# Sharing the second layer's modulation among VectorE and TensorE, and regrouping the products of a scan step

## The chip, the cores and the metric

One core of one Trainium2 chip runs the whole program in one launch. The metric is the device time of one execution in microseconds. A core has TensorE (PE; its weight loads are shown apart as PEld), VectorE (DVE), ScalarE (ACT), GpSimd (POOL) and SyncE (SP), each with a queue of its own; transfers between HBM and SBUF are issued from the queues of SP and ScalarE here.

## The reference

Two layers, with different weights, over 384 tokens of width 1024: 128 context tokens and 256 latent tokens. Each layer is a mixer and a feed-forward, and both are modulated by a condition vector `c` (one for the context, one for the latents):

```python
m = silu(c) @ w_mod + b_mod                # w_mod: 1024 x 6144, per layer
sh_m, sc_m, gt_m, sh_f, sc_f, gt_f = split(m, 6)
h = rms_norm(x) * (1 + sc_m) + sh_m
x = x + gt_m * rms_norm(mixer(h))          # four branches; one is a recurrent scan
h = rms_norm(x) * (1 + sc_f) + sh_f
f = (silu(h @ w_gate) * (h @ w_up)) @ w_down   # hidden width 2816
x = x + gt_f * rms_norm(f)
```

The scan of one mixer branch runs, per token, over a 64 x 64 state `S` per head and direction:

```python
s_a = S @ (-kk)
S = S * w + outer(s_a, kk * a) + outer(v, k)
y = S @ r
```

## The kernel before, in words

Activations lie with channels on the partitions and the 384 tokens along the free side. Every large product is made of three matmuls: weights and activations are split into a high part (rounded to fp32r) and a low part, and high x high, high x low and low x high are summed in PSUM (L684 to L686; the first stage of each sublayer has its own lines L706 to L708). Weights come from HBM in units of up to 512 KB into a ring of three raw buffers (`fetch`, L387); ScalarE copies each half unit to its high part (L417), VectorE or GpSimd subtracts to the low part (L419), four halves ahead of their use. The order of all units is a list made in advance (`layer_plan`).

A layer goes: first products of the mixer; a gate stage of 32 gate tiles (b, m), in which two side programs, attention and the scan, are woven between the gate products slot by slot (`run`, `paced`); the output projection; a bridge (norm and residual); the feed-forward's loop over 22 tiles, of which the first three are made in the bridge and tiles 3 to 21 in `ffn_main`, each a gate product, an up product and `hidden` (L1762 to L1767); the down projection (`out_gemm`, eight tiles, evacuated at L1548 and L1551); and a bridge.

The modulation is 48 output tiles of 128 rows per layer (eight tiles for each of the six parts). Layer 0's tiles 0 to 39 are made on TensorE: 0 to 15 at the start, and 16 to 39 in mixer 0, one step after each of the first 24 gate tiles, each 128 of the 1024 inputs of eight tiles (`mod_step`, `mod_mm` L515): four fp32 matmuls, 32 columns of `c` standing, 256 columns of raw weights moving, each of two passes. After eight steps ScalarE copies the bank (L542), and two steps later two transposes (L549) and an add of the bias (L553) put it in place. Such a unit sits in the ring of raw weights like any other.

The other 56 tiles (layer 0's 40 to 47 and all 48 of layer 1) are made on VectorE in layer 0's feed-forward: `mod_some` fetches the next n units of 512 KB through SP's queue into three buffers `rawm` and, placed behind the last instruction of the tile, multiplies the units fetched the call before with the two conditions, with a running sum (`mod_vector`, L561). It fetches two units a tile in `ffn_main` and three a tile in the down projection, until 56 are done. The conditions stand broadcast over the partitions in `cb`.

A scan works on chunks of 32 tokens, for a pair of heads at a time (two pairs a layer). Step i treats n = 4 sequences (two groups, two directions) for i < 4 and n = 2 for i >= 4. It forms `ry` from a state product (L1409, 64 x 64) and a score product (L1414, 32 x 64), for the two heads of the pair (`par`) on partitions 0 to 63 and 64 to 127, all in one PSUM bank; VectorE copies it to `rs` (L1417); a product with `qt` (L1425) gives `UV`; then the state update (L1435) and the last score (L1442). Before, the first part went sequence by sequence: for each `idx`, two state products, then two score products. An fp32 matmul is two passes.

Of the kernel before, what the change touches and what calls it, by code (L numbers as in the profile page):

```python
# [18 lines left out]
L = 2  # L19
# [27 lines left out]
REST = (5, 6, 7, 7)  # L47
YORD = (0, 1, 2, 3, 5, 4, 6, 7)
# [36 lines left out]
def layer_plan(l):  # L85
# [17 lines left out]
    for i in range(len(tiles) + LAG):  # L103
        if i == 8:
            for n in ("cq0", "cq1", "ckv"):
                z(n)
        if i < len(tiles):
            z("gate%d_%d" % tiles[i])
            if l == 0 and i < 24:
                mod(l, 1 + i // 16, i % 16)  # L110
        if i >= LAG:
            b, m = tiles[i - LAG]
            if m % 2 == 1:
                out.append(("br", l, (b, m // 2), 0, 2, 256))
# [136 lines left out]
def host_arrays(w):  # L251
    def by_partition(a):

        return a.reshape(*a.shape[:-1], KD, 128).swapaxes(-1, -2).reshape(a.shape)
# [5 lines left out]
    for l in range(L):  # L260
# [45 lines left out]
                         for i in range(16)]),  # L306
        "wm1": by_partition(np.concatenate([w["w_mod"][0].T.reshape(48, 128, D)[40:],
                                            w["w_mod"][1].T.reshape(48, 128, D)])),
# [17 lines left out]
def build(tc, I, O):  # L326
# [231 lines left out]
    def mod_vector(l, t, cb, acc, raw, junk):  # L558

        for g in range(2):  # L560
            V.scalar_tensor_tensor(junk, raw, 1.0, cb[:, g, :], op0=OP.mult, op1=OP.mult,  # L561
                                   accum_out=acc[:, t, g:g + 1])
# [215 lines left out]
    def mixer(l, x, xspill, hs, M, merged_of):  # L778
# [67 lines left out]
        def main():  # L846
# [9 lines left out]
            for i in range(len(tiles) + LAG):  # L856
# [3 lines left out]
                if i < len(tiles):  # L860
                    b, m = tiles[i]
                    yield from gemm(("z", l, "gate%d_%d" % (b, m)), hz, gate_evac(b, m))
                    if l == 0 and i < 24:
                        mod_step(l, 1 + i // 16, i % 16)
                        yield
# [352 lines left out]
        def rwkv_pair(pr):  # L1218
# [178 lines left out]
            for i in range(8):  # L1397
# [5 lines left out]
                for idx in range(n):  # L1403
                    g, d = IDX[idx]
                    c = chunk(g, d, i)

                    for par in range(2):
                        rows = slice(par * 64, par * 64 + 64)
                        T.matmul(ry[rows, idx, :], kr_[rows, d, c, :], sS[rows, idx, :], start=(idx == 0),  # L1409
                                 stop=False, skip_group_check=True)  # L1410
                    for par in range(2):
                        rows = slice(par * 64, par * 64 + 64)
                        lo = slice(par * 64 + 32, par * 64 + 64)
                        T.matmul(ry[rows, idx, :], am[lo, d, c, :], uv[lo, s0 + idx, :], start=False,  # L1414
                                 stop=(idx == n - 1), skip_group_check=True)
# [114 lines left out]
    def out_gemm(kind, l, xs, q, x, work, ztag, acc_tags, tags, stats=True, extra=None):  # L1530
# [40 lines left out]
        for m in range(8):  # L1571
# [8 lines left out]
            if extra:  # L1580
                extra(end[0])
# [122 lines left out]
    for l in range(L):  # L1704
# [18 lines left out]
        with tc.tile_pool(name=f"ffn{l}", bufs=1) as M:  # L1723
            if l + 1 < L:
                load_params(l + 1)
                scale_params(l + 1)
                load_rest(l + 1)
                cb = M.tile([128, 2, D], F32, name="cb")
                dma(cb, bass.AP(tensor=csd.tensor, offset=csd.offset, ap=[[0, 128], [D, 2], [1, D]]))
                acc = M.tile([128, 56, 2], F32, name="acc")  # L1730
                todo = list(range(56))

                def add_bias(l, n, t):

                    t0 = t + 1 - n
                    m0 = t0 + 40 if l == 0 else t0 - 8
                    b = PAR[l]["vec"][:, V_BMOD + m0:V_BMOD + m0 + n, None]
                    V.tensor_add(mod_tile(l)[:, m0:m0 + n, :], acc[:, t0:t + 1, :], b.to_broadcast([128, n, 2]))

                there = []  # L1740

                def mod_some(n, behind):

                    with tc.issue_after(behind.ins):
                        for t, raw in there:
                            junk = M.tile([128, D], F32, name="junk", tag="junk")
                            mod_vector(1, t, cb, acc, raw, junk)
                            if t == 7:
                                add_bias(0, 8, t)
                            elif t % 16 == 7:  # L1750
                                add_bias(1, 16, t)
                    there.clear()
                    for t in todo[:n]:
                        raw = M.tile([128, D], F32, name="rawm", tag="rawm", bufs=3)
                        dma(raw, I["wm1"][t])
                        there.append((t, raw))
                    del todo[:n]
# [13 lines left out]
            def ffn_main():  # L1771
# [5 lines left out]
                for m in range(3, FM):  # L1777
# [5 lines left out]
                    if l + 1 < L:  # L1783
                        mod_some(2, ins)

            drive(ffn_main())
            cnt["pool"] = POOL_FFN[l] - 1 if l == 0 else 1
            last = l + 1 == L
            mg, ps = out_gemm("down", l, hid, post_scale(l, 1), x, M, "z", ("sq0", "sq1", "sq2"), ("th",), not last,
                              None if last else lambda ins: mod_some(3, ins))  # L1790
# [31 lines left out]
```

## Time and profile before

| what | value |
|---|---|
| median of 3 runs | 1647.55 us (1641.81 to 1648.14) |
| the profiled execution | 1648.67 us, span 1646.9 us |
| mean granted TensorE clock | 0.974 |
| PE busy | 1563.0 us (95%), 10774 matmuls |
| DVE busy | 1065.8 us (65%) |
| ACT busy | 634.7 us (39%) |
| POOL busy | 484.1 us (29%) |
| the chain that ended last | PE 34%, DVE 5%, POOL 1% |
| modulation on VectorE (L561) | 112 x 1592 ns, 178.3 us |

Times are counted from the span's start. A matmul's shown duration overlaps with the next one's, so a cost on TensorE is read from start to start. The windows view gives, for a stretch, its length, then the busy us of PE, PEld, DVE, ACT and POOL with their instruction counts, the granted clock (1.00 is 2.4 GHz, 0.50 is 1.2 GHz), the busy share of the DMA engines and the GB/s they moved. A wait is put down to what ended it.

### The profile page before, as it was taken

To read this page: it belongs to the slowest core of one execution; us is meant where nothing else is said; L and a number is where in the kernel's file an instruction comes from. 1 tells how busy PE (TensorE), PEld (TensorE's weight loads), DVE (VectorE), ACT (ScalarE), POOL (GpSimd) and SP (SyncE) were. 2 spreads that over 40 slices of the span, in tenths; PEclk is the share of its full clock that TensorE was granted. 3 is DMA by queue.
4 is the path that set the end of the run, shared out by engine and by line. 5 is a ranking of instruction groups with operands and counts; after the bars stand their busy time and mean duration, and the time that the engine had idled before them with its cause. 6 is when DMAs were issued, how large, how long until landed. Compare 5 with 4: busy or idle time off the path is not lost. (4 is left out here: it accounts for less than half of the span.)

```text
span 1646.9 us, 28089 instructions
## 1 busy us (share of the span) xinstructions
PE 1563.0 (95%) x10774; PEld 1410.4 (86%) x10774; DVE 1065.8 (65%) x2258; ACT 634.7 (39%) x1361; POOL 484.1 (29%) x357
## 2 busy tenths in 40 slices
PE   8999999999999998888888999999999999999997
PEld 7988778777898998888888888788779999999997
DVE  5477358844567699997996586488545677444333
ACT  3463334432343432223324553344333435444331
POOL 3110001101236465553545110011112354333222
PEclk9999899999998999998999999999999979999998
DMA  9544233425541565556644442223223414333342
GB/s 334 187 136 136 67 127 112 133 84 156 161 158 59 196 215 200 195 194 203 211 161 137 128 120 82 62 83 96 74 68 119 154 61 132 128 128 128 119 128 74
DMA packets 106615, 224.25 MB, mean 136 GB/s; under 512 B 41264, under 2 KB 51568, under 8 KB 105712
## 3 DMA queue, kind: packets, MB, share of 16 engines
q1 hardware_dynamic: 79696, 136.52, 25.7%
q10 hardware_dynamic: 26784, 85.93, 16.0%
q8 instruction: 85, 1.39, 0.3%
q14 instruction: 50, 0.41, 0.1%
HBM read 213.33 MB, written 9.08 MB: 135 GB/s over the span
## 5 line engine op out<-in xcount | busy, mean ns | idle before, releaser
L417 ACT ACTIVATE whi<-raw 128x512 fp32r<-128x512 f32 (+2 forms) x580 | 343.6, 602 | 460.5 <-PE bank L685 279.7
L684 PE MATMUL bank<-hk,whi 128*128 128x384 f32 x1424 | 503.2, 354 | 1.6 <-DVE mg L1551 1.1
L685 PE MATMUL bank<-hk,whi 128*128 128x384 f32 x1424 | 483.2, 339 | 2.0 <-DVE hk L1521 2.0
L684 PEld LDWEIGHTS bank<-hk,whi 128*128 128x128 f32 x1424 | 269.6, 189 | 25.9 <-issue 15.5
L685 PEld LDWEIGHTS bank<-hk,whi 128*128 128x128 f32 x1424 | 269.7, 189 | 6.8 <-DVE hk L1521 3.2
L561 DVE SCALAR_TENSOR_TENSOR junk<-rawm,cb 128x1024 f32<-128x1024 f32 x112 | 178.3, 1592 | 0.9
L684 PE MATMUL bank<-hid,whi 128*128 128x384 f32 x352 | 121.3, 345 | 6.3 <-DVE th L1763 6.3
L685 PE MATMUL bank<-hid,whi 128*128 128x384 f32 x352 | 121.0, 344 | 0.0
L684 PEld LDWEIGHTS bank<-hid,whi 128*128 128x128 f32 x352 | 68.2, 194 | 6.6 <-DVE th L1763 6.6
L708 PE MATMUL bank<-hk,whi 128*128 128x384 f32 x192 | 62.9, 341 | 5.6 <-DVE hk L616 5.2
L685 PEld LDWEIGHTS bank<-hid,whi 128*128 128x128 f32 x352 | 68.0, 193 | 0.0
L706 PE MATMUL bank<-hk,whi 128*128 128x384 f32 x192 | 65.6, 342 | 1.9 <-ACT hk L608 1.6
L1558 POOL TENSOR_TENSOR acc<-acc,sqo 128x384 f32<-128x384 f32 x42 | 54.7, 1309 | 43.1 <-ACT sqo L1554 23.3
L1766 ACT ACTIVATE hid<-th 128x384 fp32r<-128x384 f32 x44 | 23.1, 526 | 111.5 <-DVE th L1764 110.1
L889 POOL TENSOR_TENSOR merged<-merged,gate 128x384 f32<-128x384 f32 x24 | 30.3, 1263 | 107.1 <-DVE gate L888 88.7
L1767 DVE TENSOR_TENSOR hid<-th,hid 128x384 fp32r<-128x384 f32 x44 | 36.9, 839 | 22.5 <-ACT hid L1766 22.5
L841 ACT ACTIVATE gate<-bank 128x384 f32<-128x384 f32 x64 | 31.0, 484 | 52.2 <-PE bank L686 39.9
L1417 DVE COPY rs<-bank 128x256 f32<-128x256 f32 (+1 forms) x32 | 11.5, 358 | 56.3 <-PE bank L1414 56.3
L909 ACT ACTIVATE prob<-bank,tiny 128x384 f32<-128x384 f32 (+1 forms) x56 | 27.1, 485 | 44.8 <-DVE tiny L908 42.4
L708 PEld LDWEIGHTS bank<-hk,whi 128*128 128x128 f32 x192 | 35.8, 188 | 7.9 <-DVE hk L616 6.2
L888 DVE SCALAR_TENSOR_TENSOR gate<-gate,bank 128x384 f32<-128x384 f32 x48 | 26.3, 550 | 22.9 <-PE bank L882 22.6
L706 PEld LDWEIGHTS bank<-hk,whi 128*128 128x128 f32 x192 | 36.5, 190 | 3.7 <-ACT hk L608 2.1
(2019 smaller groups left out, 3674.5 us busy)
## 6 DMA issues: line engine op xcount, KB each, us to landing
raw<-in_w ACTq DMA_DIRECT2D x126, 512.0 KB, 3.6
raw<-in_w SPq DMA_DIRECT2D x108, 512.0 KB, 3.9
rawm<-in_wm SPq DMA_DIRECT2D x56, 512.0 KB, 3.6
raw<-in_w SPq DMA_DIRECT2D x41, 384.0 KB, 3.1
wm<-in_wm SPq DMA_DIRECT2D x16, 512.0 KB, 8.0
raw<-in_w ACTq DMA_DIRECT2D x32, 256.0 KB, 2.7
raw<-in_w ACTq DMA_DIRECT2D x15, 384.0 KB, 3.4
bt<-in_bt SPq DMA_DIRECT2D x8, 256.0 KB, 4.5
```

The costliest lines, as they stand in the source:

```text
L417: last_split[:] = [S.activation(hi[:, :w], raws[i][:, sl], AF.Copy)]
L561: V.scalar_tensor_tensor(junk, raw, 1.0, cb[:, g, :], op0=OP.mult, op1=OP.mult, accum_out=acc[:, t, g:g + 1])
L684: T.matmul(ps[:, :n], wh, xh, start=(k == 0), stop=False)
L685: T.matmul(ps[:, :n], wh, xl, start=False, stop=False)
L706: T.matmul(o, wh, xh, start=(i == 0), stop=False)
L708: T.matmul(o, wh, xl, start=False, stop=(i == 7))
L841: S.activation(gates[b, m], ps[:, :NT], AF.Tanh, scale=0.5)
L888: V.scalar_tensor_tensor(gt, gt, 1.0, ps[:, :NT], op0=OP.add, op1=OP.mult)
L889: (G if m % 2 else V).tensor_add(merged[:, m, :], merged[:, m, :], gt)
L909: S.activation(e[:, :n], src, AF.Exp, bias=nb, scale=scale, accum_out=sm)
L1558: (V if i == 1 else G).tensor_add(a, a, b)
L1767: last = V.tensor_sub(h[:, 1, :], th, h[:, 0, :].bitcast(F32))
```

## The change

The modulation of layer 1 is shared out. VectorE keeps 32 tiles: in layer 0's feed-forward layer 0's 40 to 47 and layer 1's 0 to 15, in layer 1's feed-forward layer 1's 40 to 47. Layer 1's tiles 16 to 39 are made on TensorE in mixer 1, by the same steps as layer 0's in mixer 0; their units now stand in the ring of raw weights. `mod_some` fetches two units at every third tile of `ffn_main` and one at the others, and no longer runs in the down projection. In a scan step all state products are issued first, then all score products.

```diff
+VMOD = [(0, m) for m in range(40, 48)] + [(1, m) for m in range(16)] + [(1, m) for m in range(40, 48)]
+VMOD_IN = (range(0, 24), range(24, 32))
...
-            if l == 0 and i < 24:
+            if i < 24:
                 mod(l, 1 + i // 16, i % 16)
...
-                    if l == 0 and i < 24:
+                    if i < 24:
                         mod_step(l, 1 + i // 16, i % 16)
                         yield
...
-                for idx in range(n):
-                    g, d = IDX[idx]
-                    c = chunk(g, d, i)
-
-                    for par in range(2):
-                        rows = slice(par * 64, par * 64 + 64)
-                        T.matmul(ry[rows, idx, :], kr_[rows, d, c, :], sS[rows, idx, :], start=(idx == 0),
-                                 stop=False, skip_group_check=True)
-                    for par in range(2):
-                        rows = slice(par * 64, par * 64 + 64)
-                        lo = slice(par * 64 + 32, par * 64 + 64)
-                        T.matmul(ry[rows, idx, :], am[lo, d, c, :], uv[lo, s0 + idx, :], start=False,
-                                 stop=(idx == n - 1), skip_group_check=True)
+                todo = [(idx, IDX[idx][1], chunk(*IDX[idx], i), par) for idx in range(n) for par in range(2)]
+                for idx, d, c, par in todo:
+                    rows = slice(par * 64, par * 64 + 64)
+                    T.matmul(ry[rows, idx, :], kr_[rows, d, c, :], sS[rows, idx, :], start=(idx == 0),
+                             stop=False, skip_group_check=True)
+                for idx, d, c, par in todo:
+                    rows = slice(par * 64, par * 64 + 64)
+                    lo = slice(par * 64 + 32, par * 64 + 64)
+                    T.matmul(ry[rows, idx, :], am[lo, d, c, :], uv[lo, s0 + idx, :], start=False,
+                             stop=(idx == n - 1), skip_group_check=True)
...
-                todo = list(range(56))
...
+            todo = list(VMOD_IN[l])
...
+                for t in todo[:n]:
+                    raw = M.tile([128, D], F32, name="rawm", tag="rawm", bufs=3)
+                    dma(raw, I["wm1"][t])
+                    there.append((t, raw))
+                del todo[:n]
...
-                    if l + 1 < L:
-                        mod_some(2, ins)
+                    mod_some(2 if m % 3 == 0 else 1, ins)
...
-            mg, ps = out_gemm("down", l, hid, post_scale(l, 1), x, M, "z", ("sq0", "sq1", "sq2"), ("th",), not last,
-                              None if last else lambda ins: mod_some(3, ins))
+            mg, ps = out_gemm("down", l, hid, post_scale(l, 1), x, M, "z", ("sq0", "sq1", "sq2"), ("th",), not last)
```

## Rows read from the trace of the kernel before

**Rows 1.** windows: length, busy PE, PEld, DVE, ACT, POOL; clock, DMA, GB/s

```profile
577.67:585.99 8.32, 8.32 (x50) 8.32 (x49) 7.69 (x12) 3.33 (x8) 5.30 (x3) 1.00 0.63 201
577.67:741.92 164.25, 144.94 (x790) 140.71 (x788) 154.10 (x194) 49.05 (x98) 92.26 (x48) 0.97 0.58 201
741.92:763.30 21.38, 15.13 (x72) 14.88 (x71) 16.42 (x24) 5.50 (x11) 5.51 (x4) 0.76 0.63 208
763.30:846.50 83.20, 73.67 (x398) 71.45 (x397) 79.59 (x109) 26.23 (x49) 42.91 (x28) 0.96 0.60 199
1402.76:1535.88 133.12, 133.12 (x770) 133.12 (x769) 57.04 (x80) 54.96 (x98) 41.65 (x32) 1.00 0.38 126
1535.88:1551.60 15.72, 15.72 (x92) 15.72 (x91) 6.07 (x9) 5.75 (x12) 2.60 (x2) 1.00 0.34 102
1551.60:1621.30 69.70, 69.70 (x398) 69.70 (x397) 22.45 (x39) 23.74 (x44) 15.12 (x14) 1.00 0.38 123
```

**Rows 2.** tanh of the gate/up loop, each layer: count, ns, first and last start

```profile
L1762 ACT ACTIVATE th<-bank x17: 468/472/474, 577.7 to 741.9; 128x384 f32<-128x384 f32 x17
...
L1762 ACT ACTIVATE th<-bank x17: 472/472/472, 1402.8 to 1535.9; 128x384 f32<-128x384 f32 x17
```

**Rows 3.** TensorE's waits, layer 0 feed-forward: total us, times, longest

```profile
PE bank L684 <- DVE th L1763: 6.3, 1, 6.3
PE bank L686 <- DVE wlo__8214 L419: 2.5, 1, 2.5
```

**Rows 4.** modulation products: groups of instructions (busy, mean ns), and their durations

```profile
L561 DVE SCALAR_TENSOR_TENSOR junk<-rawm,cb 128x1024 f32<-128x1024 f32 x112 | 178.3, 1592 | 0.9
...
L561 DVE DVE_READ_ACCUMULATOR junk<-rawm,cb 128x1 f32 x112 | 8.8, 78 | 0.0
...
L561 DVE SCALAR_TENSOR_TENSOR junk<-rawm,cb x112: 1208/1219/2329, 575.3 to 859.9; 128x1024 f32<-128x1024 f32 x112
```

**Rows 5.** windows view: gate stages of mixers 0 and 1, a stretch of 0

```profile
144.10:469.70 325.60, 320.78 (x2616) 257.70 (x2617) 183.59 (x480) 118.76 (x269) 45.28 (x36) 0.98 0.41 124
991.30:1294.00 302.70, 297.28 (x2434) 249.64 (x2433) 181.62 (x483) 116.21 (x266) 45.82 (x37) 1.00 0.29 87
174.11:184.35 10.24, 10.24 (x65) 8.02 (x62) 3.63 (x10) 2.92 (x7) 0.00 (x0) 0.50 0.08 27
```

**Rows 6.** TensorE in order of time, a modulation step: start us, us, count

```profile
158.22 0.33 PE L685 MATMUL bank<-hk,whi 128*128 128x384 f32 x1
158.39 0.34 PE L686 MATMUL bank<-hk,wlo__1832 128*128 128x384 f32 x1
158.66 0.64 PE L515 MATMUL bank<-raw,cs 128*32 128x256 f32 x8
159.23 0.45 PE L684 MATMUL bank<-hk,whi 128*128 128x384 f32 x1
```

**Rows 7.** transposes of the modulation in mixer 0: count, duration ns min/median/max

```profile
L549 PE MATMUL bank<-cst,mt x6: 271/273/329, 276.8 to 437.4; 128*128 128x128 f32 x6
```

**Rows 8.** TensorE in order of time, one scan step of four products

```profile
154.88 0.33 PE L1409 MATMUL bank<-S,KR 64*64 64x64 f32 x4
155.14 0.33 PE L1414 MATMUL bank<-UV,AM 32*64 32x64 f32 x4
...
156.97 0.45 PE L684 MATMUL bank<-hk,whi 128*128 128x384 f32 x1
```

**Rows 9.** TensorE in order of time, blocks of one kind, 16 and 8 passes

```profile
1023.08 0.68 PE L1435 MATMUL bank<-UV,BKT 64*64 64x64 f32 x16
1023.69 0.63 PE L1442 MATMUL bank<-UV,AM 32*32 32x64 f32 x14
...
213.52 0.45 PE L1435 MATMUL bank<-UV,BKT 64*64 64x64 f32 x8
213.90 0.41 PE L1442 MATMUL bank<-UV,AM 32*32 32x64 f32 x8
```

**Rows 10.** ScalarE's waits in mixer 0's gate stage: total us, times, longest

```profile
ACT whi L417 <- DMA raw<-in_w: 24.9, 16, 4.8
```

More of the change, by code (lines that the diff above doesn't have):

```diff
@@ L306, in host_arrays @@
                          for i in range(16)]),
-        "wm1": by_partition(np.concatenate([w["w_mod"][0].T.reshape(48, 128, D)[40:],
-                                            w["w_mod"][1].T.reshape(48, 128, D)])),
+        "wm1": np.stack([by_partition(w["w_mod"][l].T.reshape(48, 128, D)[m]) for l, m in VMOD]),
         "x": x.T.reshape(KD, 128, NT).transpose(1, 0, 2),
@@ L556, in mod_place, with mod_vector @@
         return last
-    def mod_vector(l, t, cb, acc, raw, junk):
+    def mod_vector(t, cb, acc, raw, junk):
         for g in range(2):
@@ L1528, in drive, with out_gemm @@
             pass
-    def out_gemm(kind, l, xs, q, x, work, ztag, acc_tags, tags, stats=True, extra=None):
+    def out_gemm(kind, l, xs, q, x, work, ztag, acc_tags, tags, stats=True):
         ps2, ps3 = bk_rw(), bk_o()
@@ L1579, in out_gemm @@
                     sums(6)
-            if extra:
-                extra(end[0])
         with tc.issue_after(main_mm[0].ins):
@@ L1727, in build @@
                 load_rest(l + 1)
-                cb = M.tile([128, 2, D], F32, name="cb")
-                dma(cb, bass.AP(tensor=csd.tensor, offset=csd.offset, ap=[[0, 128], [D, 2], [1, D]]))
-                acc = M.tile([128, 56, 2], F32, name="acc")
-                todo = list(range(56))
[L1733 to L1757, printed above, removed]
+            cb = M.tile([128, 2, D], F32, name="cb")
@@ new lines, in build, with add_bias, mod_some @@
+            dma(cb, bass.AP(tensor=csd.tensor, offset=csd.offset, ap=[[0, 128], [D, 2], [1, D]]))
+            acc = M.tile([128, len(VMOD), 2], F32, name="acc")
+            todo = list(VMOD_IN[l])
+            def add_bias(t):
+                (ml, m0), t0 = VMOD[t - 7], t - 7
+                b = PAR[ml]["vec"][:, V_BMOD + m0:V_BMOD + m0 + 8, None]
+                V.tensor_add(mod_tile(ml)[:, m0:m0 + 8, :], acc[:, t0:t + 1, :], b.to_broadcast([128, 8, 2]))
+            there = []
+            def mod_some(n, behind):
+                with tc.issue_after(behind.ins):
+                    for t, raw in there:
+                        junk = M.tile([128, D], F32, name="junk", tag="junk")
+                        mod_vector(t, cb, acc, raw, junk)
+                        if t % 8 == 7:
+                            add_bias(t)
+                there.clear()
+                for t in todo[:n]:
[3 more added lines that the diff above has]
+                del todo[:n]
@@ L1782, in ffn_main @@
                     ins = hidden(m, *got)
-                    if l + 1 < L:
-                        mod_some(2, ins)
+                    mod_some(2 if m % 3 == 0 else 1, ins)
             drive(ffn_main())
+            assert not todo and not there
             cnt["pool"] = POOL_FFN[l] - 1 if l == 0 else 1
             last = l + 1 == L
-            mg, ps = out_gemm("down", l, hid, post_scale(l, 1), x, M, "z", ("sq0", "sq1", "sq2"), ("th",), not last,
-                              None if last else lambda ins: mod_some(3, ins))
+            mg, ps = out_gemm("down", l, hid, post_scale(l, 1), x, M, "z", ("sq0", "sq1", "sq2"), ("th",), not last)
             if last:
```

## The prediction, made before the change was run

> **What bounds the kernel now.** I read the page's engine shares and clock line first, then cut the span into stages with the windows view, then compared the same stage of the two layers, then the waits of TensorE, and last the instructions in order of time. The two layers run the same program on the same shapes, so one layer's stage is a measured stand-in for the other's.
>
> The two feed-forward stages differ most [rows 1, 2]. From the fourth to the last gate/up tile there are 17 tanh instructions, so 16 tiles, in both layers. Layer 1 takes 133.1 us, 8.32 us a tile, TensorE busy without a hole and VectorE 57.0 us. Layer 0 takes 164.3 us, 10.27 us a tile, VectorE busy 154.1 us: 9.63 of each 10.27. The down projection repeats it: 21.38 us to its first tile against 15.72, then 83.20 us for six tiles against 69.70. TensorE's waits in these stages name VectorE each time: one of 6.3 us for `th`, and ten of 1.9 to 2.5 us for a low half of the weights (L419), of which the longest is shown [rows 3]. So in layer 0 VectorE sets the pitch, and what fills it is the modulation: 112 products of 1.59 us, each with an accumulator read of 0.08 us, 1.67 us together [rows 4]. In layer 1's feed-forward TensorE sets the pitch.
>
> In the gate stage of both mixers TensorE sets it: busy 320.8 of 325.6 us in layer 0, 297.3 of 302.7 us in layer 1 [rows 5]. An instruction added there costs its time, one removed gives it back, less what then waits.
>
> **The change part by part.** The sum is made against the profiled execution, 1648.67 us (span 1646.9, 1.8 us around it); the median of the runs is 1647.55, 1.1 lower.
>
> (a) *Gate/up of layer 0.* The loop fetched 38 units of two products; now it fetches 24: two at every third tile, one at the others, and multiplies them a tile later. A tile now carries 4 products, 6.68 us of VectorE's 9.63, which leaves 2.95 for its own work. Afterwards three tiles carry 8 products, 13.4 us, and 3 x 2.95 = 8.9: 22.2 us against 3 x 8.32 = 25.0 of TensorE. The one tile in three that keeps four products asks for 9.63, 1.3 us over the pitch; the two after it ask for 6.29 and leave 2.0 each. That such an overhang is swallowed is seen in the first tile that carried four products: VectorE did 7.69 of the 9.63 asked, and the tile still took 8.32 [rows 1]. So TensorE's pitch returns and the stage takes 133.1: **-31.1 us**. Late next is TensorE itself. If the cover failed in every one of the six heavy tiles, 6 x 1.3 = 8 us would come back: bounds -31.1 and -23.
>
> (b) *Down projection of layer 0.* Its 18 units go altogether, with the two left over from the loop. The stretch to the first tile falls by 5.7 us, the next six tiles by 13.5: **-19.2 us**. The last tile is left as it is, since it carried no product. The layer-0 stage also squares and sums for the next norm, which layer 1 doesn't; that may keep 2 us of it: bounds -19.2 and -17.
>
> (c) *Modulation in mixer 1.* 24 steps of four matmuls (eight passes) are added, and three pairs of transposes, three copies on ScalarE and three small adds on VectorE. In mixer 0 the same step lies between an L686 that begins at 158.39 and an L684 at 159.23, 0.84 us where two neighbouring matmuls are 0.17 apart (158.22 to 158.39): 0.67 us a step, 24 x 0.67 = 16.1 [rows 6]. Six transposes at 0.27 us add at most 1.6 [rows 7]. That makes 17.7. From above: mixer 0's gate stage is 22.9 us longer than mixer 1's [rows 5], but it holds a stretch of 10.24 us at a granted clock of 0.50, the lower level, 1.2 GHz, which costs at most half of itself, 5.1; 22.9 - 5.1 = 17.8. I take **+18.0**, bounds 16.1 (transposes hidden) and 22.9. The 24 transfers of 512 KB move from SP's queue to ScalarE's, where each waits until TensorE has read the unit three before it. Queued behind it are the copies that split the weights and the evacuations of PSUM, and TensorE waits for both. In mixer 0, which has the same order, ScalarE waits 24.9 us for such transfers in 16 waits [rows 10], yet TensorE is busy 98.5% of the stage; so I cost the move at nothing beyond the 22.9. SP loses 32 transfers in layer 0 and gains 8 in layer 1.
>
> (d) *Order in the scan step.* A step of four products reads state, score, state, score, eight blocks, from 154.88 to the next matmul at 156.97: 2.09 us, 0.26 a block, and so 1.04 us for the four blocks of a two-product step [rows 8]. Blocks of one kind run closer: 16 passes of L1435, the same 64x64 shape, take 0.61 us from start to the next kind, 8 passes 0.38 [rows 9]. The 32x64 scores have no such row; the nearest are L1435 and the 32x32 L1442, 14 passes of which last 0.63 us where 16 of L1435 last 0.68, so I take 0.61 and 0.38 for them too. A four-product step then takes 1.22 us, 0.87 less, a two-product step 0.76, 0.28 less. There are 16 of each (two pairs of heads, two layers): 13.9 + 4.5 = 18.4 us. Between blocks VectorE and ScalarE work for the attention side, and they lose up to 0.87 us of cover a step; I give a tenth back: **-16.5**, bounds -18.4 and nothing (the instructions are the same, so no loss).
> Here a rule speaks against the change. The Trainium skill, TensorEngine Tiling (Array Packing), section Gotcha 1: PSUM Pressure, says that different row tiles cannot access one PSUM bank at the same time; the two heads of a pair are such row tiles, and here they write one bank. By it grouping would overlap nothing and (d) would be about nothing. The L1435 rows disagree: its passes write one bank at 0.61/16 = 0.04 us each, the mixed blocks at 0.26/4 = 0.065.
>
> (e) *Feed-forward of layer 1.* Eight units, 16 products, 26.7 us of VectorE, are added within the first seven tiles of the loop, with their bias and one broadcast of the condition. VectorE asks 57.0/16 = 3.6 us a tile there [rows 1]; with four products 10.2, twice, 1.9 over the pitch, with two 6.9. Covered as in (a): **+0.5**, bounds 0 and 2 x 1.9 = 3.8.
>
> Sum: -31.1 - 19.2 + 18.0 - 16.5 + 0.5 = -48.3. 1648.67 - 48.3 = 1600.4; less the 1.1 to the median, 1599.3. I say **1600 us**.
>
> **Rivals.** *R1, the regrouping gives nothing*, because the switch of tile shape is not what spaces the blocks, or because other waits take the time back. For it: the 32x64 shape was never seen in a row of its own kind. Against it: rows 8 and 9. 1600 + 16.5 = 1616.
>
> *R2, mixer 1 takes the whole price of mixer 0*, with a stretch at the lower clock: +22.9 instead of 18.0, 1605. For it: mixer 0 has such a stretch where scan, attention and modulation meet. Against: one of two head pairs there had it.
>
> *R3, VectorE and GpSimd still hold each other up in layer 0.* The products took 1.21 us at best, 2.33 at worst [rows 4]; L561 alone loses 0.38 us a product in the mean. If a light tile kept all of a saturated tile's delays, it would ask 10.27 - 2 x 1.29 = 7.7 us and a heavy one 10.27: 25.7 for three tiles, 8.55 a tile, 16 x 0.23 = 3.7 us back; with the bound of (a), 8. 1604 to 1608. The Trainium skill, SBUF — State Buffer, section Who interferes with whom, says that a VectorE instruction with two SBUF inputs and a GpSimd instruction that reads SBUF exclude each other for the whole instruction; the spread of L561 agrees with it, and by it the time would be that of this rival.
>
> *R4, slower: the weight ring starves in mixer 1.* Each modulation unit takes one of three raw buffers, so at each the next weights are fetched later. If each of the 24 held TensorE up for the longest wait that ScalarE had for such a transfer in mixer 0, 4.8 us [rows 10]: 24 x 4.8 = 115 in place of 18, 1600 + 97 = 1697. It decides against the change from (48.3 + 18) / 24 = 2.8 us a step. Against: mixer 0 pays 22.9 / 24 = 0.95 with the same ring.
>
> **How the numbers follow.** Forecast 0.61 (own range 1590 to 1609), R1 0.10, R2 0.12, R3 0.12, R4 0.03, with 0.02 for no change at all, by some mix of these. Low end: cheapest (c), all of (d) and the lower clock gone from mixer 0: -31.1 - 19.2 + 16.1 - 18.4 - 5.1 = -57.7, 1590, and 2 us below for the spread of the runs: 1588. High end: R1 with two of R3's microseconds, 1618. A measurement of this kernel can tell 0.5% from no change, 8.2 us. All but R4 and the last case lie below 1639: faster 0.95, same 0.02, slower 0.03.
>
> **What would show it.** Layer 0's tiles at 8.32 us and no wait of TensorE for L419 there (a); its six down tiles at 70 us (b); mixer 1's gate stage at 302.7 + 18 less half of (d), about 312, and mixer 0's at about 317 (c, d); one block of 16 L1409 and one of 16 L1414, 0.61 us each (d); layer 1's 16 tiles still at 133 us (e). Wrong if TensorE waits for VectorE after heavy tiles, if L1414 stays at 0.26 us a pair, or if mixer 1 grows by more than 23 us before (d).

## The result, and the profile after

The changed kernel takes 1597.95 us (median of 4 runs, 1594.01 to 1600.84) against 1647.48 for the kernel before (median of 4): ratio 0.9705 [0.9672, 0.9738]. The profiled execution took 1600.84 us, its span 1599.1, so 47.8 us less than the span before. Cut into the stages of [rows 1, 5], they are found here; the first seven lines answer to those rows, the last two are needed below. An output projection, in the table, runs from its first evacuation (L1548) to its last.

Windows view of the changed kernel; columns as in [rows 1]: mixer 0's gate stage, the 16 tiles of layer 0's gate/up loop, the stretch to the first down tile, six down tiles, mixer 1's gate stage, layer 1's 16 tiles and six down tiles, then one stretch in each mixer.

```profile
144.75:458.63 313.88, 308.85 (x2616) 250.93 (x2616) 183.50 (x479) 118.85 (x269) 45.41 (x36) 0.99 0.43 129
566.13:699.25 133.12, 133.12 (x770) 133.12 (x769) 102.80 (x155) 54.30 (x97) 77.02 (x48) 1.00 0.64 208
699.25:715.02 15.77, 15.77 (x92) 15.77 (x91) 8.66 (x16) 5.74 (x11) 5.59 (x4) 1.00 0.40 120
715.02:784.73 69.71, 69.71 (x398) 69.71 (x397) 27.93 (x41) 26.25 (x50) 34.03 (x28) 1.00 0.39 126
928.30:1247.80 319.50, 312.51 (x2634) 251.83 (x2628) 185.21 (x488) 117.71 (x270) 45.54 (x37) 0.99 0.41 121
1354.98:1488.10 133.12, 133.12 (x770) 133.12 (x769) 77.87 (x112) 54.71 (x98) 46.13 (x33) 1.00 0.44 146
1503.81:1573.51 69.70, 69.70 (x398) 69.70 (x397) 22.46 (x39) 23.73 (x43) 15.13 (x14) 1.00 0.39 124
...
170.00:188.00 18.00, 18.00 (x251) 13.79 (x250) 9.81 (x27) 6.18 (x17) 1.28 (x1) 1.00 0.19 58
1085.37:1092.20 6.83, 6.83 (x24) 3.88 (x22) 5.42 (x21) 1.96 (x5) 0.00 (x0) 0.50 0.11 40
```

| stage | before | after | difference | forecast |
|---|---|---|---|---|
| mixer 0, gate stage | 325.60 | 313.88 | -11.7 | -8.25 |
| its output projection | 34.98 | 33.94 | -1.0 | 0 |
| layer 0, 16 gate/up tiles | 164.25 | 133.12 | -31.1 | -31.1 |
| to the first down tile, six down tiles | 104.6 | 85.5 | -19.1 | -19.2 |
| its last down tile | 13.70 | 13.26 | -0.4 | 0 |
| mixer 1, gate stage | 302.70 | 319.50 | +16.8 | +9.75 |
| its output projection | 34.23 | 33.09 | -1.1 | 0 |
| layer 1, 16 gate/up and six down tiles | 202.8 | 202.8 | 0.0 | +0.5 |

The whole of the gain in layer 0's feed-forward stands in the second to fourth lines: TensorE is busy without a hole at a granted clock of 1.00; in the 16 tiles it had been busy 88% of the time at 0.97 [rows 1]. In the same stretches no wait of TensorE is left, neither for L419's `wlo` nor for `th` [rows 3]. The tanh instructions start 8.32 us apart in both layers now, 17 of them in 133.2 us, which answers to [rows 2].

Instructions of one tile, changed kernel: tanh of both layers (count, duration in ns, first and last start).

```profile
L1757 ACT ACTIVATE th<-bank x17: 469/470/472, 566.1 to 699.3; 128x384 f32<-128x384 f32 x17
...
L1757 ACT ACTIVATE th<-bank x17: 471/472/472, 1355.0 to 1488.1; 128x384 f32<-128x384 f32 x17
```

VectorE's products fell from 112 to 64, and in the mean from 1592 to 1460 ns. The shortest is as before, 1210 ns against 1208 [rows 4]. Fewer are held up: 18 of the 64 took over 1.3 us, 46 of the 112 before. Beside each of the 18, and each of the 46, a tensor instruction of GpSimd was running; the 46 others of the change took at most 1.23 us, and half of them had one beside them for less than 0.1 us.

Groups of instructions, changed kernel (busy us, mean ns | idle before).

```profile
L563 DVE SCALAR_TENSOR_TENSOR junk<-rawm,cb 128x1024 f32<-128x1024 f32 x64 | 93.4, 1460 | 0.5
```

The scan step, which was eight blocks in 2.09 us [rows 8], is two. In order of time on TensorE, changed kernel (start us, length us, passes): a step of four products, then one of two.

```profile
155.47 0.68 PE L1409 MATMUL bank<-S,KR 64*64 64x64 f32 x16
156.08 0.68 PE L1414 MATMUL bank<-UV,AM 32*64 32x64 f32 x16
156.69 0.44 PE L686 MATMUL bank<-hk,whi 128*128 128x384 f32 x1
...
208.32 0.45 PE L1409 MATMUL bank<-S,KR 64*64 64x64 f32 x8
208.70 0.45 PE L1414 MATMUL bank<-UV,AM 32*64 32x64 f32 x8
209.08 0.49 PE L939 MATMUL bank<-z,z 64*128 64x256 f32 x2
```

From 155.47 to 156.69 is 1.22 us, from 208.32 to 209.08 is 0.76: both as forecast from [rows 9].

Two stages are off: mixer 1 is 7 us above its forecast, mixer 0 3.4 us below. In mixer 1 ScalarE waits for weights as it did in mixer 0 [rows 10]:

Waits of ScalarE, changed kernel, mixer 1's gate stage (us in total, times, longest).

```profile
ACT gate L843 <- PE bank L688: 31.3, 20, 3.4
ACT whi L419 <- DMA raw<-in_w: 30.7, 16, 5.7
```

### The profile page after: what moved, and what is told of

It is laid out like the page before. It is cut to its first block, busy times and chain, and to the rows that moved or that the text cites. A ratio compares the mean times of both kernels' runs of the same rounds, so it can differ in the third digit from the quotient of the medians.

```text
span 1599.1 us, 28341 instructions
## 1 busy us (share of the span) xinstructions
PE 1546.4 (97%) x10972; PEld 1393.3 (87%) x10972; DVE 972.0 (61%) x2165; ACT 640.6 (40%) x1364; POOL 461.7 (29%) x357
## 3 DMA queue, kind: packets, MB, share of 16 engines
q10 hardware_dynamic: 30240, 98.51, 19.2%
## 5 line engine op out<-in xcount | busy, mean ns | idle before, releaser
L419 ACT ACTIVATE whi<-raw 128x512 fp32r<-128x512 f32 (+2 forms) x580 | 346.0, 603 | 495.8 <-PE bank L687 269.4
L686 PE MATMUL bank<-hid,whi 128*128 128x384 f32 x352 | 119.2, 339 | 0.0
L687 PE MATMUL bank<-hid,whi 128*128 128x384 f32 x352 | 119.0, 338 | 0.0
L563 DVE SCALAR_TENSOR_TENSOR junk<-rawm,cb 128x1024 f32<-128x1024 f32 x64 | 93.4, 1460 | 0.5
L686 PEld LDWEIGHTS bank<-hid,whi 128*128 128x128 f32 x352 | 66.2, 188 | 0.0
L687 PEld LDWEIGHTS bank<-hid,whi 128*128 128x128 f32 x352 | 66.2, 188 | 0.0
L1558 POOL TENSOR_TENSOR acc<-acc,sqo 128x384 f32<-128x384 f32 x42 | 51.5, 1237 | 31.7 <-ACT sqo L1548 15.7
L843 ACT ACTIVATE gate<-bank 128x384 f32<-128x384 f32 x64 | 31.1, 486 | 64.9 <-PE bank L688 57.4
L1762 DVE TENSOR_TENSOR hid<-th,hid 128x384 fp32r<-128x384 f32 x44 | 42.2, 959 | 22.5 <-ACT hid L1761 22.5
L1759 DVE SCALAR_TENSOR_TENSOR th<-th,bank 128x384 f32<-128x384 f32 x44 | 24.3, 552 | 39.4 <-PE bank L688 39.0
L1551 DVE TENSOR_SCALAR mg<-bank,Q 128x128 f32<-128x128 f32 x64 | 23.6, 409 | 31.9 <-ACT sqo L1548 30.7
```

Of the source, the lines that this page charges most:

```text
L419: last_split[:] = [S.activation(hi[:, :w], raws[i][:, sl], AF.Copy)]
L686: T.matmul(ps[:, :n], wh, xh, start=(k == 0), stop=False)
L687: T.matmul(ps[:, :n], wh, xl, start=False, stop=False)
L843: S.activation(gates[b, m], ps[:, :NT], AF.Tanh, scale=0.5)
L1558: (V if i == 1 else G).tensor_add(a, a, b)
L1762: last = V.tensor_sub(h[:, 1, :], th, h[:, 0, :].bitcast(F32))
```

## The experiments

All times are medians; stages are of the profiled execution of each kernel.

**One part at a time.** First the changed kernel with the scan step's old order, so the modulation alone:

```diff
-                for idx, d, c, par in todo:
-                    rows = slice(par * 64, par * 64 + 64)
...
+                for idx in range(n):
...
+                    for par in range(2):
+                        rows = slice(par * 64, par * 64 + 64)
...
```

> The sharing of the modulation alone, with the scan step in its old order. My theory of additive parts: layer 0's loop of 16 tiles at 133.1 us and its six down tiles at 69.7 us, as in the changed kernel (together 50 us less than before), scan blocks at 2.09 us, mixer 0's gate stage at 325.6 us as before, and mixer 1's at 302.7 plus the price of the 24 steps: 320 to 321 by my 18 us, 328 to 329 if the 26 us that the changed kernel's stage seems to hold (319.5 - 302.7 + 9.2) is their true price. Time: 1647.5 - 50 + 18 = 1615, or 1623 by the 26. Rival (the regrouping gave nothing or little, the saving came from VectorE alone): 1598 to 1602.

Measured 1626.32 us, ratio 0.9881 [0.9854, 0.9909]. The feed-forwards came out as in the whole change (133.12 and 69.70 us). The mixers did not. Windows view, modulation alone: both gate stages, and a stretch in mixer 1.

```profile
144.38:473.42 329.04, 322.51 (x2616) 258.97 (x2616) 183.51 (x479) 118.86 (x269) 45.05 (x36) 0.98 0.41 123
942.81:1272.92 330.11, 324.16 (x2634) 258.88 (x2627) 185.16 (x487) 117.79 (x270) 45.52 (x37) 0.98 0.40 117
990.25:1003.90 13.65, 13.65 (x90) 9.75 (x85) 4.58 (x14) 2.77 (x8) 0.00 (x0) 0.50 0.26 64
```

Mixer 1 grew by 27.4 us [rows 5], where 18 was expected by the sum and 26 by the first profile of the change. 13.65 us of it ran at a granted clock of 0.50, the lower level; if that costs half of itself, 6.8, the added work costs 20.6. Mixer 0, which should have stayed at 325.6, took 3.4 us more; it has a second stretch of 3.41 us at 0.50, at 424 us, worth about 1.7 of them.

Then the kernel before with the new order alone:

```diff
+                todo = [(idx, IDX[idx][1], chunk(*IDX[idx], i), par) for idx in range(n) for par in range(2)]
+                for idx, d, c, par in todo:
+                    rows = slice(par * 64, par * 64 + 64)
...
```

> The regrouping of the scan step alone, with the modulation as before. My theory: blocks of 1.22 and 0.76 us, each mixer's gate stage 9.2 us shorter at most, 16 to 18 us in all, so 1630 to 1632; 2 to 3 us more if mixer 0 loses its stretch at the lower clock, as it did in the changed kernel. The feed-forwards stay at 164.3 and 133.1 us. Rival (the blocks get shorter but the time is given back as waits on VectorE and ScalarE): 1640 to 1647, with new TensorE waits in the gate stages.

Measured 1629.12 us, ratio 0.9900 [0.9869, 0.9932], as expected with mixer 0's stretch at the lower clock gone. Windows view, new scan order alone: both gate stages, and layer 0's 16 tiles, which are untouched.

```profile
144.05:456.19 312.14, 307.22 (x2616) 249.26 (x2616) 183.49 (x479) 118.52 (x269) 45.31 (x36) 1.00 0.43 129
976.20:1270.34 294.14, 288.10 (x2434) 244.69 (x2433) 182.11 (x483) 116.32 (x266) 45.76 (x37) 1.00 0.31 89
562.52:726.73 164.21, 144.87 (x781) 140.72 (x780) 154.07 (x194) 49.16 (x97) 92.08 (x48) 0.96 0.59 201
```

Mixer 1 gives 8.6 us, close to half of the 16.5. Mixer 0 gives 13.5, and its clock reads 1.00: the 10.24 us at 0.50 of [rows 5] are gone, worth up to 5.1. By the shorter blocks alone a mixer would give half of 18.4, 9.2 us; of the 0.6 missing in mixer 1 TensorE's idle time shows all, 294.14 - 288.10 = 6.0 us against 5.4 before. So other waits take back less than a tenth there, and R1's second reason falls.

**Why the blocks run closer.** In layer 0 all state products by head, then all scores by head; in layer 1 two state products (both heads), their scores, and so on:

```diff
+                if l == 0:
+                    parts = [sorted(todo, key=lambda e: e[3])]
+                else:
+                    parts = [todo[k:k + 4] for k in range(0, len(todo), 4)]
+                for part in parts:
+                    for idx, d, c, par in part:
...
```

> The changed kernel with other orders of the same products. Layer 0: all state products of the first head, then of the second, then all scores the same way. Layer 1: two sequences' states, two sequences' scores, and again. If each switch of the tile shape costs a fixed time (theory), layer 1's four-product step is two of the two-product steps of the changed kernel, 2 x 0.755 = 1.51 us, and its two-product step stays at 0.755. If what counts is that the two heads overlap although they write one PSUM bank, layer 0's step gets longer than 1.22 us: with one pass each 0.052 us (two passes of one tile in the rows are 0.05 apart) 32 x 0.052 + 0.15 = 1.8 us. By the Trainium skill, TensorEngine Tiling (Array Packing), Gotcha 1: PSUM Pressure, the two heads could not have overlapped, and layer 0's step stays at 1.22 us. Time: 1600 + 16 x 0.3 + 0.6 x 8 + 0.3 x 8 = about 1607.

One run, 1610.92 us. In order of time on TensorE, two orders: a four-product step of layer 0, then one of layer 1.

```profile
155.17 0.96 PE L1414 MATMUL bank<-S,KR 64*64 64x64 f32 x16
156.06 0.96 PE L1419 MATMUL bank<-UV,AM 32*64 32x64 f32 x16
156.95 0.44 PE L686 MATMUL bank<-hk,whi 128*128 128x384 f32 x1
...
973.14 0.45 PE L1414 MATMUL bank<-S,KR 64*64 64x64 f32 x8
973.52 0.45 PE L1419 MATMUL bank<-UV,AM 32*64 32x64 f32 x8
973.90 0.45 PE L1414 MATMUL bank<-S,KR 64*64 64x64 f32 x8
974.28 0.45 PE L1419 MATMUL bank<-UV,AM 32*64 32x64 f32 x8
```

Two things are told apart. With the heads one after the other, 16 passes take 0.89 us; with the heads by turns, 0.61. So by turns some of one head's work runs under the other's, though both write one bank of PSUM. What runs under what stays open. The Trainium skill, TensorEngine Tiling (Array Packing), section Gotcha 1: PSUM Pressure, says that different row tiles cannot access one bank at the same time; no run here shows whether these do. By turns a pass of 64 columns costs 0.03 us in the mean, and at the pace of the large products, 384 columns in 0.17 us [rows 6], 64 columns would take 0.028 us by themselves, as an estimate. It may then be only one head's weight load that lies under the other's pass. And with the heads by turns, each switch of kind costs: blocks of 4, 8 and 16 passes take 0.26, 0.38 and 0.61 us, so 0.03 us a pass and about 0.15 us for the switch.

**What mixer 1 pays.** The 24 steps without their transfers, reading a tile that is resident, so that parts 16 to 39 of layer 1's modulation are not those of the reference:

```diff
-            if i < 24:
+            if l == 0 and i < 24:
...
+        if l == 1:
+            mod_mm(mod_ps[l, sg], PAR[l]["small"][:, :1024], half, k)
```

> The changed kernel, but mixer 1's 24 steps read a resident tile of small weights in place of their own weights, so their units take no place in the ring and no transfer on ScalarE's queue; the modulation of layer 1's parts 16 to 39 is therefore not that of the reference. If the ring and its transfers are what lifts the price of the steps from 18 to 26 us, mixer 1's gate stage falls from 319.5 to about 311 us and the time to about 1590. If it is what the 24 more slots bring together (the sides meet other gate tiles, a stretch at the lower clock), the stage stays at 317 to 321 us and the time at 1596 to 1600.

Measured 1592.72 us (1591.88 to 1596.34), ratio 0.9681 [0.9657, 0.9705]. Windows view, no fetch: mixer 1's gate stage.

```profile
926.11:1237.94 311.83, 307.25 (x2630) 251.21 (x2627) 180.54 (x488) 117.84 (x269) 45.78 (x37) 0.99 0.29 84
```

311.83 - 302.70, and the 8.6 that the scan order gives back: the bare steps cost 17.7, the +18 of the prediction. It is less still, 16.0, if one takes off half of a stretch of 3.41 us at the lower clock that this execution had, at 1076 us. So 24 x 0.67 = 16.1 fits, and the rest comes with fetching the weights.

The fetches of mixer 1's modulation units on SP's queue in place of ScalarE's:

```diff
-            queue.dma_start(r[:, :cols], dap(I["w"], offs[i], [[cols, 128], [1, cols]]))
+            (nc.sync if PLAN[i][:2] == ("mod", 1) else queue).dma_start(r[:, :cols], dap(I["w"], offs[i], [[cols, 128], [1, cols]]))
```

> The changed kernel with the 24 modulation units of mixer 1 issued from SP's queue; they keep their places in the ring of three raw buffers. Without any fetch mixer 1's gate stage fell from 319.5 to 311.8 us. If those 8 us came from ScalarE's queue standing still while such a transfer waits for its buffer, with the weight copies and evacuations behind it, the stage falls to 312 to 315 us and the time to 1592 to 1594. If they came from the ring's places (the weights behind a modulation unit are fetched one place later and land late), the stage stays at 317 to 321 us, 1596 to 1600.

Measured 1595.45 us (1594.36 to 1604.21), ratio 0.9699 [0.9663, 0.9735]: not to be told from the changed kernel. Windows view and waits of ScalarE, units by SP, mixer 1's gate stage.

```profile
928.54:1241.79 313.25, 305.26 (x2634) 248.84 (x2634) 183.82 (x488) 118.55 (x270) 45.58 (x37) 1.00 0.42 123
...
ACT whi L419 <- DMA raw<-in_w: 42.2, 22, 5.6
```

ScalarE's waits for weights did not go away with the queue, they rose from 30.7 us in 16 to 42.2 in 22, and the stage took 313.25 us. So these waits are not made by the order on ScalarE's queue alone. The stage lies where the queue was expected to be the cause, but the unaltered change, in its second profile below, took 314.80, and the median lies between the two expectations: the run does not decide between queue and ring. The three places of the ring remain as a possible cause; a fourth was not tried.

The order of the work in mixer 1 is set by two paces; here layer 1 takes layer 0's:

```diff
-PACE_RW, PACE_AT = (1.14, 1.12), (1.3, 1.5)
+PACE_RW, PACE_AT = (1.14, 1.14), (1.3, 1.3)
```

> The changed kernel with layer 0's paces of the two side programs in mixer 1 too (1.14 and 1.3 instead of 1.12 and 1.5): attention's steps come closer together. If the last microseconds of mixer 1 hang on which side step meets which gate tile, its stage moves by 3 us or more to either side of 319.5 (mixer 0 needed 313.9 in the changed kernel with these paces, so 314 is the guess). If they hang on the ring, the stage stays within 3 us of 319.5.

Measured 1598.16 us (1594.97 to 1600.65), ratio 0.9701 [0.9680, 0.9722]. Windows view, layer 0's pace: mixer 1's gate stage.

```profile
926.71:1241.85 315.14, 307.92 (x2616) 248.23 (x2616) 185.18 (x479) 118.61 (x268) 45.63 (x37) 1.00 0.41 122
```

The median shows no difference. The stage is 4.4 us shorter than in the first profile of the change, but as long as in the second (314.80, below), so the pace is not what moved it.

**How far VectorE can be filled.** Eight of the 24 steps go back to VectorE, as eight units of two products: two more at the end of layer 0's loop and one at each of six tiles of its down projection:

```diff
+VMOD = [(0, m) for m in range(40, 48)] + [(1, m) for m in range(16)] + [(1, m) for m in range(32, 48)]
+VMOD_IN = (range(0, 32), range(32, 40))
+MSTEPS = (24, 16)
...
-            if i < 24:
+            if i < MSTEPS[l]:
...
+                              None if last else lambda ins: mod_some(1, ins))
```

> Tiles 32 to 39 of layer 1 (the feed-forward's scale) go from TensorE in mixer 1 back to VectorE: 8 units, two fetched at the last tile of layer 0's loop and one at each of six down tiles. Theory: VectorE has the room there (a down tile asks 3.3 us of it without products, 6.6 with one unit, of TensorE's 11.65), so layer 0's loop stays at 133.1 and its six down tiles at 69.7 us, and mixer 1 loses a third of its steps. By the 26 us that 24 steps cost with their fetches: 319.5 - 8.7 = 311 us and 1589; by 18 us, 313.5 and 1592. Rival (in the down stage VectorE also sums for the norm, and any product there costs): down tiles over 70.5 us, 1594 to 1600.

Measured 1587.56 us (1585.92 to 1591.09), ratio 0.9640 [0.9619, 0.9662]: faster than the change, by intervals that do not overlap. Windows view, sixteen steps: layer 0's 16 tiles, its six down tiles, mixer 1's gate stage.

```profile
565.14:698.26 133.12, 133.12 (x770) 133.12 (x769) 102.90 (x155) 54.32 (x97) 77.54 (x48) 1.00 0.65 210
713.86:782.50 68.64, 68.64 (x398) 68.64 (x397) 47.30 (x69) 26.23 (x50) 37.40 (x28) 1.00 0.52 166
925.25:1234.56 309.31, 304.31 (x2568) 249.09 (x2567) 183.17 (x486) 118.23 (x267) 45.62 (x37) 1.00 0.38 111
```

Mixer 1 is 10.2 us shorter than in the change (5.5 against its second profile, below). The down tiles hide the products altogether (VectorE 47.3 of 68.6 us). They even take 1.06 us less than without them, in layer 1 too, where nothing was added: that is taken up below.

Then sixteen of the 24 steps go back, two units at every second tile of the loop and at each down tile:

```diff
+VMOD = [(0, m) for m in range(40, 48)] + [(1, m) for m in range(32)] + [(1, m) for m in range(40, 48)]
+VMOD_IN = (range(0, 40), range(40, 48))
+MSTEPS = (24, 8)
...
+                    mod_some(2 if (m % 2 if l == 0 else m % 3 == 0) else 1, ins)
...
+                              None if last else lambda ins: mod_some(2, ins))
```

> Also tiles 16 to 31 of layer 1 on VectorE; mixer 1 keeps 8 steps (tiles 32 to 39). Layer 0's loop fetches two units at odd tiles and one at even ones, and two at each of six down tiles. VectorE is asked for 10.0 + 2 x 2.95 = 15.9 us in two tiles of the loop, of TensorE's 16.64, and 3.3 + 6.7 = 10 of 11.65 in a down tile. If the ask decides (theory), the loop stays at 133.1 and the down tiles at 69.7, mixer 1's stage is 319.5 - 17 = 302 and the time 1581. If GpSimd's holding up of VectorE's two-input products counts (R3 of the prediction), the loop grows by some us: with every second tile heavy, (10.27 + 7.7)/2 = 8.98 a tile, 144 us, and the time is about 1592.

Measured 1603.47 us (1599.79 to 1604.18), ratio 0.9730 [0.9710, 0.9749]: above the change by 5.5 us of the medians, though the intervals of the two ratios overlap, and far above both expectations. Windows view, eight steps: the same three stages.

```profile
566.57:705.02 138.45, 135.94 (x780) 134.66 (x779) 123.69 (x163) 51.60 (x98) 87.58 (x48) 1.00 0.62 209
726.34:802.77 76.43, 70.44 (x398) 68.34 (x397) 66.83 (x91) 26.26 (x49) 41.67 (x28) 1.00 0.56 181
945.80:1250.49 304.69, 296.13 (x2502) 248.25 (x2503) 185.34 (x485) 117.57 (x267) 45.39 (x37) 0.99 0.35 99
```

Waits of TensorE, eight steps, layer 0's feed-forward.

```profile
PE bank L687 <- DVE th L1761: 4.5, 1, 4.5
PE bank L689 <- DVE wlo__8176 L422: 1.5, 1, 1.5
```

VectorE is busy for less than TensorE's own time in both stages (123.7 of 133.1 us, 66.8 of the 68.6 that six down tiles take in layer 1 here), and they still grow, by 5.3 and 7.8 us, with another 5.6 in the stretch to the first down tile: the waits of [rows 3] are back. That outweighs the 10 us by which mixer 1 is shorter than in the change's second profile. A product took 1544 ns in the mean here, 1490 with sixteen steps, 1460 in the change, with 1.21 us the least in each; 38 of the 96 took over 1.3 us, each with a tensor instruction of GpSimd beside it. With VectorE busy for 77% of TensorE's time in the loop the delays are swallowed, with 93% they are not.

**The lowest medians.** Sixteen steps, with the units by SP, and that with layer 0's pace for both mixers:

```diff
+            (nc.sync if PLAN[i][:2] == ("mod", 1) else queue).dma_start(r[:, :cols], dap(I["w"], offs[i], [[cols, 128], [1, cols]]))
```

```diff
-PACE_RW, PACE_AT = (1.14, 1.12), (1.3, 1.5)
+PACE_RW, PACE_AT = (1.14, 1.14), (1.3, 1.3)
```

> The kernel with sixteen steps in mixer 1 (1587.6 us), its 16 modulation units issued from SP's queue. With 24 units the change of queue was worth 2.5 us of the medians and 6 us of the stage. If the queue counts by the unit: 1585 to 1586, mixer 1's stage 305 to 308 us. If what remains at sixteen units is the steps' own time, 1587 to 1589.

> The same, and layer 0's paces of the side programs in mixer 1 as well. With 24 steps the pace alone moved the median by 0.2 us and the stage by -4.4, of which up to 3.4 are a stretch at the lower clock that it had not: I expect 1584 to 1587, no difference that the interval shows.

Measured 1585.05 us (1579.79 to 1592.27), ratio 0.9637 [0.9611, 0.9663], and 1586.61 (1583.71 to 1592.51), ratio 0.9639 [0.9614, 0.9663]. Windows view, sixteen steps by SP: mixer 1's gate stage.

```profile
926.80:1232.53 305.73, 298.78 (x2568) 247.49 (x2569) 182.60 (x486) 118.37 (x267) 45.85 (x37) 1.00 0.38 112
```

In the last of them the stage took 311.10 us, with a stretch of 6.83 us at 0.50 in it. All three kernels with sixteen steps are alike within their spread, so neither the queue nor the pace shows, and each is below the change.

**A stage that changed without being touched.** The six down tiles took 68.64 us with sixteen steps and 69.70 in the change, in both layers. Besides the work, one tile that stands beside the weights in SBUF had grown, from 32 columns to 40. That alone:

```diff
-            acc = M.tile([128, len(VMOD), 2], F32, name="acc")
+            acc = M.tile([128, 40, 2], F32, name="acc")
```

> The changed kernel, where only the tile of the running sums `acc` is made 40 columns long instead of 32; the 8 more are never written, so only the addresses of the tiles after it change. In the two kernels with a longer `acc` (40 and 48) six down tiles took 68.64 us in both layers, where before and after the change they took 69.70. If the addresses make that, they take 68.64 here too, 2.4 us less in all, and the rest stays as in the changed kernel. If it came from the products in the down stage or the other lists, they stay at 69.70.

One run, 1594.73 us. Windows view, the change with 40 columns: the gate stages of mixers 0 and 1, and six down tiles in both layers.

```profile
143.58:461.30 317.72, 311.45 (x2616) 252.28 (x2616) 183.64 (x479) 118.86 (x270) 45.46 (x36) 0.98 0.42 127
927.50:1241.42 313.92, 308.84 (x2630) 250.06 (x2627) 185.67 (x487) 117.91 (x270) 45.28 (x37) 1.00 0.42 123
716.21:784.85 68.64, 68.64 (x398) 68.64 (x397) 28.03 (x41) 26.23 (x50) 34.49 (x28) 1.00 0.41 126
1498.92:1567.56 68.64, 68.64 (x398) 68.64 (x397) 22.55 (x39) 23.75 (x43) 15.10 (x14) 1.00 0.40 126
```

The addresses do it, then: six tiles of 66 matmuls, 173.3 ns each, against 176.0 in the mean. Of the 10.4 us by which the median with sixteen steps lies below that of the change, 2 x 1.06 are theirs, 5.5 are mixer 1's against the second profile of the change, and the rest is not assigned to a stage.

The first line also prices the lower clock. Mixer 0's gate stage took 312.1 to 312.6 us in the four profiles with the new scan order that have no stretch at 0.50 in it (the scan order alone, no fetch, layer 0's pace, sixteen steps by SP), 313.8 to 314.7 in six with one of 3.41 us, and 317.7 here, with one of 10.24: about half of what each stretch lasts.

**The change again**, unaltered, to see how much of mixer 1 belongs to the one execution:

> The changed kernel once more, unaltered, for a second profile. In the first, mixer 1's gate stage took 319.5 us with a stretch of 6.8 us at the lower clock in it; the same program with other addresses took 313.9 without one. If the clock (and what an execution happens to meet) makes that, the second profile has 313 to 316 us without such a stretch, and 317 to 320 with one, and the median stays at 1596 to 1599 us. If the addresses make it, 319 without one too.

Measured 1596.95 us (1595.88 to 1600.52), ratio 0.9714 [0.9687, 0.9741]. Windows view, the change again: mixer 1's gate stage and layer 0's six down tiles.

```profile
927.58:1242.38 314.80, 309.31 (x2634) 249.99 (x2627) 185.26 (x487) 118.05 (x269) 45.34 (x37) 1.00 0.41 123
714.03:783.73 69.70, 69.70 (x398) 69.70 (x397) 27.98 (x41) 26.25 (x50) 34.20 (x28) 1.00 0.39 125
```

The same stage is 4.7 us shorter than in the first profile, and its clock reads 1.00: the 6.83 us at 0.50 that stand there at 1085 are not in this one. Half of them is 3.4; the other 1.3 us are open.

## Why the prediction was right, step by step

The forecast was 1600 us within 1588 to 1618, the median 1597.95. In the profiled execution -47.8 us stand against -48.3. That the two agree to half a microsecond is luck: mixer 1 came out 7.1 us above its term, mixer 0 3.4 below, the two output projections 2.2, (e) 0.5 and the last down tile 0.4.

(a) and (b), layer 0's feed-forward: shown, -31.1 and -19.1 us. The way to them was to read layer 1's stage as the measured floor of layer 0's, and it was met to 0.1 us. The overhang of 1.3 us of the heavy tiles was swallowed as assumed. R3's price is out for this kernel, since its pitch of 8.55 would be 3.7 us more. Its mechanism shows all the same: every product that took over 1.3 us had GpSimd beside it. But VectorE was busy for only 3 x 102.80/16 = 19.3 us in three tiles, where (a) had asked for 22.2. With eight steps VectorE's delays reach TensorE again; what they would be without GpSimd was not tried.

Two readings of the rows were off. The 17 tanh instructions run from the sixth of the 22 tiles, not from the fourth; nothing hangs on it, since both layers are cut alike. And the last down tile did carry products: [rows 4] has their last start at 859.9 us. Windows view, kernel before: that tile.

```profile
846.50:860.20 13.70, 13.36 (x85) 13.04 (x84) 13.67 (x20) 2.91 (x7) 8.03 (x5) 1.00 0.47 153
```

TensorE waited 0.3 us there for a low half from VectorE; that wait is gone, and it is most of the tile's 0.4.

(c), mixer 1: the term that was mis-sized. The first profile shows 16.8 + 8.6 = 25.4 us, above the 23 that the prediction named as a sign of being wrong. Four other executions, with no stretch at the lower clock in that stage, give 19.1 (units by SP), 19.8 (40 columns), 20.7 (the change again) and 21.0 (layer 0's pace). So the steps themselves cost 16.0 to 17.7, the low half of the term's range, and fetching their weights another 1.4 to 5, which I had costed at nothing within the bound of 22.9. A stretch at the lower clock adds about half of what it lasts in the executions that have one, 3.4 in the first profile. By medians the fetch is worth 4 to 5 us (1592.72 against 1596.95 and 1597.95), but the runs' ranges overlap, and so do the intervals of the ratios. R2 is half right: the clock stretch comes in some executions, but the other gains cover it. R4 falls: ScalarE waits for weights for 30.7 us, up to 5.7 at a time, but TensorE's idle time in the stage is 319.50 - 312.51 = 7.0 us against 5.4 before.

(d), the scan order: shown, by the blocks to the hundredth (1.22 and 0.76 us), by the median of that part alone, and mixer 1's 8.6 us. The tenth that I gave back was about right: 0.6 of 9.2 us in mixer 1. Whether both heads use one bank at the same time, as the step takes the rows of L1435 to say, the two orders leave open; the gain does not hang on it. What the step missed is mixer 0: 3.4 us more than its half. The 10.24 us at the lower clock went too, worth 5.1, and a new stretch of 3.41 came, worth 1.7: that is the 3.4. I had the first in the low end of the range only.

(e), layer 1's feed-forward: 0.0, where +0.5 was taken; TensorE busy 133.12 of 133.12 us.

Not forecast are 2.2 us in the two output projections. They lie in the last tile of each (8.38 to 7.52 us, 8.73 to 7.58), and they go with the clock: of these tiles the last 3.53 and 2.67 us ran at 0.50 in the kernel before, 1.74 and nothing in the change, and half of the differences is 0.9 and 1.3. In the second profile of the change the two projections took 34.46 and 34.58 us, so this is no gain to count on.

Open: how the price of the fetch divides between the ring's places and ScalarE's queue (the run with the units on SP was inside the spread), and why an execution of mixer 1 has a stretch at the lower clock and the next has none.

## What to carry to other kernels

Where two layers run one program and only one carries extra work, the other's stage is the floor that the first returns to, and moving work is worth the difference down to that floor and no more. Work that has to go somewhere is cheapest as cover under an engine that is already full, up to the point where that cover's own delays show (here VectorE held when busy for 77% of TensorE's time in the loop and failed at 93%), so the best split tried, sixteen steps in mixer 1, lay between that of the change and an even bigger share on VectorE. Small matmuls of one tile shape are worth bringing together, with the two heads by turns.

## What was not expected of the hardware

*The clock falls without a hole.* In the kernel before, TensorE was busy 10.24 of 10.24 us while 0.50 was granted [rows 5], the lower of its two levels, and busy at 1.00 ahead of it. Windows view, kernel before: the stretch that ends where the clock fell.

```profile
165.00:174.11 9.11, 9.11 (x108) 6.07 (x106) 4.17 (x11) 2.67 (x7) 1.29 (x1) 1.00 0.36 115
```

In the three kernels whose layer-0 scan steps take 1.78 or 2.09 us (before, the modulation alone, the order by head) this stretch stands at about 174 us; in the eleven profiles with steps of 1.22 us it is absent. That goes with the order of the small matmuls; what in it the clock answers to was not tried. It is not the only such stretch: with 40 columns one stands at 322 us, in the change one at 1085, and six of the eleven have one of 3.41 us at about 410, TensorE busy throughout. Windows view, changed kernel.

```profile
409.55:412.96 3.41, 3.41 (x12) 3.41 (x12) 0.86 (x2) 0.93 (x2) 0.00 (x0) 0.50 0.73 179
```

*The pitch of a matmul depends on where its operands lie.* The same 6 x 66 matmuls of the down projection took 68.64 or 69.70 us by the size of one tile allocated ahead of their operand `hid`, 1.5% with the same work and the same clock. Which addresses are the good ones was not tried.

*Two heads by turns cost less than one after the other, in one PSUM bank.* 16 passes took 0.61 us by turns, 0.89 one after the other; what overlaps in them is open.
